# Gates of a token block: which PSUM buffers they use, and in which order gates, norm rows, output transposes and hidden splits are written

## The chip, the cores and the metric

The kernel runs on one core of one Trainium2 chip. The metric is the device time of one launch in microseconds (us), lower is better; the runs shown give its median.

## The reference, cut to what matters

One decoder layer for 1024 prompt rows and 32 sampled rows (8 sequences of 4), 1056 token rows in all, D_MODEL = 1024, D_FF = 2816. Attention, a state-space branch and their merge come first and are not touched here. What follows is:

```
up = rmsnorm(x, g_ffn) @ w_up
conv = conv_b + sum of three taps of up along the sequence
a, v = split(conv)
x = x + (gelu(a) * v) @ w_down
x = x + sigmoid(rmsnorm(x, g_ple) @ w_ple_gate) * (p @ w_ple_proj)
```

The last rows of `up` before the convolution are outputs as well (conv_prompt, conv_sample). All matrix products are done to fp32 accuracy.

## The kernel before, in words

**Products.** An fp32 operand is split in two fp32r parts, hi = round(x) and lo = x - hi. ACT casts the hi part (line 82), DVE or POOL subtracts (line 83). `mm3` (lines 85 to 88) then issues three matmuls per 128x128 weight tile: hi-hi, hi-lo, lo-hi. Activations lie transposed, features on partitions and tokens on columns.

**Up.** For each of 22 pairs of feature tiles, `up_pair` makes seven products (in the sequence `ORDER`), adds them to the quarters of `up`, runs the convolution and the gelu, and writes the hidden rows to the DRAM tensor `dhid` (`middle`). In the last pair `last_pair` begins to read the hidden rows of the first token block back: `hid_split(b, g, eng)` splits group g (three feature tiles, 128x1056; group 7 has one, 128x352) of block b into its fixed M tiles. Group 6 is called after the product m = 4, group 7 after the last pair's convolution and gelu.

**Blocks.** The tokens are cut in three blocks of 352 columns. `block(b)` does all of a block's remaining work:

- `down(o, kgs)`: for each of eight output tiles o, 22 feature tiles in six groups kg of four (the last of two), accumulated in a PSUM tile `pd` of the pool `psDn` (three buffers). `down_out` adds the residual (DVE, line 2157), scales by g_ple and splits into `GG[o]` (ACT 2160, DVE 2161), and adds the square to `sqb` (ACT 2166; POOL, or DVE for o = 7, 2167). In block 0 outputs 0 and 1 are interleaved.
- `gate(o)`: 8 k-tiles of `GG` in two groups kg, 24 matmuls, into a PSUM tile `pu` of the pool `psU` (three buffers).
- `sums` (line 2196): column sums of `sqb` by six small matmuls, then the reciprocal root on DVE (`rst`). `rows` (2208, 2209): transposes `rst` to a row on all partitions, which DVE copies to `rb`.
- `rest(o)`: DVE multiplies the gate by `rb` (2222), ACT takes the sigmoid (2223), DVE multiplies by the projected p in `pe[o]` and adds the residual (2224, 2225). The result is `y`.
- `out_turn(o)`: three transposes on TensorE into a tile `pt` of the pool `psP` (two buffers), two copies to SBUF on ACT (2234, 2236), and two DMA issues on ACT's queue (2235, 2238); a third (2240) in the last block.
- `hid_split(b + 1, o, V)` after gate o: the hidden rows of the next block.

In the order of the program: gate 0, sums, gate 1, rows, rest 0, rest 1, turn 0, gate 2, rest 2, turn 1, and so on. While outputs 2 and up of block 0 go through `down`, `last_rows` turns the conv rows of the outputs (lines 2125 to 2131), with one buffer for its SBUF tile `lo_`.

**Loads.** Weights and hidden rows share five SBUF buffers with the tag `raw`. `raw_load` lists the loads in order (`rseq`), `pull` issues the next one on SP's queue for each one that has been used up, so that five are loaded ahead; a hidden group is held back until its rows have been written. `raws` finds a loaded tile by its key: ("d", o, i) for a part of w_down, ("g", o) for w_ple_gate, ("h", b, g) for hidden rows. In the list, gate weights and hidden groups alternate: g0, h0, g1, h1, to g7, h7, then the next block's w_down.

**Weight units.** `units` lists the half loads in the order of their use, `dn_unit` splits one, and `ahead` keeps three split units in `wq` before TensorE's use of them. The split tiles have four buffers. The subtraction alternates between POOL and DVE.

**What sets the order.** The program's order is a priority. A planner issues on each engine the first instruction whose operands are ready and whose buffer is free in its own model of the times, and fixes the sequence of every engine's queue by that; each engine then works through its queue in that sequence and waits where an operand is late. So an instruction may stand on its engine ahead of others that the program names earlier.

Of the kernel before, what the change touches and what calls it, by code (L numbers as in the profile page):

```python
# [9 lines left out]
F32 = mybir.dt.float32  # L10
# [11 lines left out]
BLK = T // 3  # L22
# [33 lines left out]
def body(tc, I, O):  # L56
# [8 lines left out]
    with ctx:  # L65
# [1620 lines left out]
        units = []  # L1686
        for b in range(3):
            kgs = [(o, kg) for o in range(8) for kg in range(6)]
            if b == 0:
                kgs = [(o, kg) for q in (range(4), (4, 5)) for o in range(2) for kg in q] + kgs[12:]  # L1690
            units += [("d", o, kg) for o, kg in kgs] + [("g", o, kg) for o in range(8) for kg in range(2)]

        for b in range(3):
            if b == 0:
                for x in ("h0", (0, 0), "h1", "h2", (0, 1), "h3", "h4", "h5", "h6", (1, 0), (1, 1), (0, 2), "h7", (1, 2)):
                    if x[0] == "h":
                        hid_raw(0, int(x[1]))
                    else:
                        dn_load(*x)
            for o in range(2 if b == 0 else 0, 8):  # L1700
                for i in range(3):
                    dn_load(o, i)
            for o in range(8):
                raw_load(("g", o), k8(), w_pg[:, :, cols_(o)])
                if b < 2:
                    hid_raw(b + 1, o)

# [387 lines left out]
        def last_pair(m):  # L2095
            if m in ORDER[:6]:
                g = ORDER.index(m)
                hid_split(0, g, V if g % 2 else G)
            if m == 4:
                hid_split(0, 6, V)  # L2100
# [3 lines left out]
        while post:  # L2104
            step()
        hid_split(0, 7, V)
        pX.close()
# [16 lines left out]
        def last_rows(q):  # L2124
            pt = ps.tile([128, 512], F32, name="pt")
            for j in range(4):
                PE.transpose(pt[:18, j * 128:(j + 1) * 128], LU[:, q + j], ident)
            lo_ = p2.tile([18, 512], F32, name="lo_", bufs=1)
            A.copy(lo_, pt[:18])
# [5 lines left out]
        def block(b):  # L2135
# [10 lines left out]
            def p_in(o):  # L2146
                pe[o] = btile("pe", 3)
                SP.dma_start(pe[o], dpp[cols_(o), c])
# [34 lines left out]
            if b == 0:  # L2183
                for kgs in (range(4), (4, 5)):
                    for o in range(2):
                        down(o, kgs)
            for o in range(2 if b == 0 else 0, 8):
                down(o, range(6))
# [21 lines left out]

            def gate(o):
                pg_ = psu.tile([128, BLK], F32, name="pu")
                for kg in range(2):
                    wt = wq.pop(0)
                    ahead()
                    for k in range(4 * kg, 4 * kg + 4):
                        mm3(pg_, wt[:, 0, k % 4], wt[:, 1, k % 4], GG[k][:, 0], GG[k][:, 1], k == 0, k == 7)
                return pg_

            def rest(o, pg_):  # L2220
                y = Y[o] = btile("y", 3)
                V.tensor_tensor(y, pg_, rb, OP.mult)
# [18 lines left out]

            pgs = {}
            p_in(0)
            p_in(1)
            for o in range(8):
                pgs[o] = gate(o)
                if b < 2:
                    hid_split(b + 1, o, V)
                if o == 0:
                    rst = sums()  # L2250
                    continue
                if o == 1:
                    rows(rst)
                    rest(0, pgs.pop(0))
                rest(o, pgs.pop(o))
                if o < 7:
                    p_in(o + 1)
                out_turn(o - 1)
            out_turn(7)
# [44 lines left out]
```

## Time and profile before

| | us |
|---|---|
| median of 3 runs | 2057.62 |
| lowest, highest | 2054.71, 2059.20 |
| the profiled execution, its own time | 2064.64 |
| its span, from the first to the last instruction | 2062.8 |
| its mean granted TensorE clock, as a share of full speed | 0.968 |

All rows below come from the one profiled execution; times count from the start of its span. PE is TensorE's matmuls, DVE VectorE, ACT ScalarE, POOL GpSimd, SP the queue that issues most loads; a q behind an engine's name is its sequencer, which issues DMAs. `raw<-dhid` reads: into the tile raw, from dhid. In a timeline a row gives start, duration, engine, line of the kernel, operation, tiles and shapes, and in brackets how long the engine had been idle and what released it. A matmul row of 0.32 us overlaps the next one's by half. In these rows the up stage ends at about 1673 us, and the three blocks end at about 1814, 1938 and 2063 us.

### The profile page before, as it was taken

The numbers are of one execution on the slowest core, as the hardware profiler recorded it, in microseconds if no ns is written. First come the engines' busy times: TensorE is split into PE (matmuls) and PEld (weight loads), VectorE is DVE, ScalarE is ACT, GpSimd is POOL, SyncE is SP. The second block draws the span as 40 slices with busy tenths as digits, with TensorE's granted clock in tenths as the row PEclk, the third lists the DMA queues.
The fourth block names the chain that finished last, engine by engine and source line by source line (L and its number), as shares of the span: only waits on it lengthen the run. The fifth ranks groups of instructions, "written<-read, shape, count | busy, mean of one in ns | idle before, by whom it ended". The sixth has DMA issues, their size and how long they took to land.

```text
span 2062.8 us, 35870 instructions
## 1 busy us (share of the span) xinstructions
PE 1958.3 (95%) x13329; PEld 1839.7 (89%) x13329; DVE 1255.5 (61%) x2467; ACT 920.8 (45%) x1910; POOL 870.2 (42%) x926
## 2 busy tenths in 40 slices
PE   7998999999998989999999899999999989999998
PEld 6897888888777768888999899999999989999998
DVE  6517542335787856565553878787878773734524
ACT  5412332243665544455333454444444454544543
POOL 1106341101323222212442668787878754344342
PEclk9999999998999979999999999999999999999999
DMA  7402221243321100003356432322232274766743
GB/s 250 127 15 59 66 70 55 72 115 110 104 58 45 45 1 12 2 1 139 109 148 214 124 131 63 94 63 94 63 94 63 94 212 139 219 188 180 225 138 102
DMA packets 291927, 211.53 MB, mean 103 GB/s; under 512 B 38417, under 2 KB 273092, under 8 KB 291754
## 3 DMA queue, kind: packets, MB, share of 16 engines
q1 hardware_dynamic: 275102, 195.86, 32.0%
q10 hardware_dynamic: 16652, 13.39, 2.0%
q8 instruction: 105, 1.72, 0.3%
q14 instruction: 68, 0.56, 0.1%
HBM read 161.07 MB, written 46.78 MB: 101 GB/s over the span
## 4 chain that ended last, share of the span: by engine, by line
PE 74%; DVE 10%; ACT 2%; DMA 2%; POOL 2%; issue 2%; SPq 0%; ACTq 0%; DVEq 0%; POOLq 0%
PE q L2014 21%; PE pd L87 4%; PE pd L88 4%; PE pd L86 4%; PE q L1941 3%; PE pm L88 3%; PE pm L87 3%; PE pm L86 3%; PE pt L86 2%; PE pv L1377 2%; PE pt L88 2%; PE pt L87 2%; PE p L86 2%; PE p L88 2%; PE p L87 2%
## 5 line engine op out<-in xcount | busy, mean ns | idle before, releaser
L2014 PE MATMUL q<-M,wx 128*128 128x264 f32 x2112 | 279.2, 285 | 2.0 <-DVE up L2034 2.0
L2014 PEld LDWEIGHTS q<-M,wx 128*128 128x128 f32 x2112 | 266.8, 188 | 2.2 <-issue 2.2
L83 POOL TENSOR_TENSOR wx<-raw,wx 128x512 fp32r<-128x512 f32 x108 | 147.9, 1371 | 226.6 <-ACT wx L82 217.1
L82 ACT CAST wx<-raw 128x512 fp32r<-128x512 f32 x226 | 133.5, 597 | 195.4 <-PE pd L88 117.1
L2014 PE MATMUL q<-P,wx 128*128 128x264 f32 x1584 | 216.0, 285 | 0.1
L2014 PEld LDWEIGHTS q<-P,wx 128*128 128x128 f32 x1584 | 200.3, 188 | 3.8 <-DVE up L2026 3.8
L83 DVE TENSOR_TENSOR wx<-raw,wx 128x512 fp32r<-128x512 f32 (+1 forms) x118 | 92.2, 783 | 141.1 <-ACT wx L82 137.6
L86 PE MATMUL pd<-M,wx 128*128 128x352 f32 x528 | 171.8, 325 | 0.0
L87 PE MATMUL pd<-M,wx 128*128 128x352 f32 x528 | 171.4, 325 | 0.0
L88 PE MATMUL pd<-M,wx 128*128 128x352 f32 x528 | 171.2, 324 | 0.0
L2057 DVE SCALAR_TENSOR_TENSOR cv<-up,cw,cv 128x1024 f32<-128x1024 f32 x88 | 142.1, 1615 | 28.3 <-ACT cv L2049 28.3
L88 PE MATMUL pm<-xh,wl 128*128 128x352 f32 x384 | 126.9, 331 | 0.0
L87 PE MATMUL pm<-xl,wh 128*128 128x352 f32 x384 | 126.5, 329 | 0.0
L86 PE MATMUL pm<-xh,wh 128*128 128x352 f32 x384 | 126.1, 328 | 0.0
L1359 POOL TENSOR_TENSOR Pt<-Pt,mstT 128x128 f32<-128x128 f32 x64 | 30.6, 480 | 176.4 <-ACT Pt L1358 176.4
L86 PEld LDWEIGHTS pd<-M,wx 128*128 128x128 f32 x528 | 100.0, 189 | 0.1
L87 PEld LDWEIGHTS pd<-M,wx 128*128 128x128 f32 x528 | 99.9, 189 | 0.0
L88 PEld LDWEIGHTS pd<-M,wx 128*128 128x128 f32 x528 | 99.9, 189 | 0.0
L1747 ACT CAST wx<-raw 128x512 fp32r<-128x512 f32 x110 | 67.9, 618 | 71.4 <-PE q L2014 46.5
L1941 PE MATMUL q<-M,wx 128*128 128x264 f32 x720 | 90.8, 286 | 5.4 <-POOL wx L83 2.6
L1941 PEld LDWEIGHTS q<-M,wx 128*128 128x128 f32 x720 | 88.3, 188 | 6.8 <-POOL wx L83 3.1
L1748 DVE TENSOR_TENSOR wx<-raw,wx 128x512 fp32r<-128x512 f32 x66 | 76.5, 1159 | 11.8 <-ACT wx L1747 11.8
(705 smaller groups left out, 5473.3 us busy)
## 6 DMA issues: line engine op xcount, KB each, us to landing
raw<-w_down SPq DMA_DIRECT2D x48, 512.0 KB
raw<-w_up SPq DMA_DIRECT2D x44, 512.0 KB
raw<-w_ple_gate SPq DMA_DIRECT2D x24, 512.0 KB
dhid<-cv SPq DMA_DIRECT2D x22, 528.0 KB
raw<-dhid SPq DMA_DIRECT2D x21, 528.0 KB
raw<-w_down SPq DMA_DIRECT2D x24, 384.0 KB
wst<-w_in SPq DMA_DIRECT2D x16, 512.0 KB
cb<-cache_ckv SPq DMA_DIRECT2D x64, 128.0 KB
```

The lines of the kernel that those rows point to most:

```text
L82: A.copy(hi, src)
L83: (eng or G).tensor_tensor(lo, src, hi.bitcast(F32), OP.subtract)
L86: PE.matmul(out, lh, rh, start=start, stop=False)
L87: PE.matmul(out, lh, rl, start=False, stop=False)
L88: PE.matmul(out, ll, rh, start=False, stop=stop_)
L1359: G.tensor_tensor(Pt[:, :128], Pt[:, :128], mstT, OP.add)
L1377: PE.matmul(W["pv"][:, j, :DV + 1], Pts[k][:, q0:q0 + 128], Vb[hp][:, k, e], start=k == 0, stop=k == i)
L1747: A.copy(w[:, 0], s)
L1748: (G if m in (2, 5, 4) else V).tensor_tensor(w[:, 1], s, w[:, 0].bitcast(F32), OP.subtract)
L1941: PE.matmul(p_[:, n, :QW], a_, b_[:, k % 4], start=k + x == 0 and kg == 0, stop=k == 7 and x == 2)
L2014: PE.matmul(o_, l_, r_, start=start and k + x == 0, stop=k + x == 5, skip_group_check=not start)
L2057: V.scalar_tensor_tensor(C[:, :S], U[:, tp:tp + S], w[tp], C[:, :S], op0=OP.mult, op1=OP.add)
```

## The change

Gates 0 and 1 are computed together, first their k-tiles 0 to 3, then 4 to 7, and the list of weight units follows. Gate 3 and gate 7 take a PSUM tile of psDn, the others of psU. The sums stand behind gates 0 and 1, the rows behind gate 3, followed by rest 0, 1 and 2. From gate 4 on, gate o is followed by rest o - 1, a hidden split of the next block and the turn of output o - 3 (for o = 4 also of output 0); the turns of outputs 5, 6 and 7 stand behind gate 7 and its rest. Hidden splits of the next block begin after rest 2, and their loads are listed accordingly: g0 to g3, h0, h1, g4, h2, g5, h3, g6, h4, g7, h5, h6, h7. In the last up pair group 6 is split after the product m = 3, and group 7 of block 0 after the first four kg of down outputs 0 and 1. `pe` and `y` get four buffers in place of three, `lo_` three in place of one, and pe[2] is loaded at the start.

```diff
@@ -1688,7 +1688,7 @@
             kgs = [(o, kg) for o in range(8) for kg in range(6)]
             if b == 0:
                 kgs = [(o, kg) for q in (range(4), (4, 5)) for o in range(2) for kg in q] + kgs[12:]
-            units += [("d", o, kg) for o, kg in kgs] + [("g", o, kg) for o in range(8) for kg in range(2)]
+            units += [("d", o, kg) for o, kg in kgs] + [("g", o, kg) for op in ((0, 1), (2,), (3,), (4,), (5,), (6,), (7,)) for kg in range(2) for o in op]
 
         for b in range(3):
             if b == 0:
@@ -1702,8 +1702,9 @@
                     dn_load(o, i)
             for o in range(8):
                 raw_load(("g", o), k8(), w_pg[:, :, cols_(o)])
-                if b < 2:
-                    hid_raw(b + 1, o)
+                for g in {3: (0, 1), 7: (5, 6, 7)}.get(o, (o - 2,) if o > 3 else ()):
+                    if b < 2:
+                        hid_raw(b + 1, g)
 
         wsum = {}
 
@@ -2096,14 +2097,13 @@
             if m in ORDER[:6]:
                 g = ORDER.index(m)
                 hid_split(0, g, V if g % 2 else G)
-            if m == 4:
+            if m == 3:
                 hid_split(0, 6, V)
 
         for j in range(NH):
             up_pair(j, first_pair if j == 0 else last_pair if j == NH - 1 else lambda m: None)
         while post:
             step()
-        hid_split(0, 7, V)
         pX.close()
         f1.close()
 
@@ -2125,7 +2125,7 @@
             pt = ps.tile([128, 512], F32, name="pt")
             for j in range(4):
                 PE.transpose(pt[:18, j * 128:(j + 1) * 128], LU[:, q + j], ident)
-            lo_ = p2.tile([18, 512], F32, name="lo_", bufs=1)
+            lo_ = p2.tile([18, 512], F32, name="lo_", bufs=3)
             A.copy(lo_, pt[:18])
             A.dma_start(cvp[:, q * 128:(q + 4) * 128], lo_[0:2])
             A.dma_start(cvs[:, q * 128:(q + 4) * 128], lo_[2:18])
@@ -2144,7 +2144,7 @@
                 SP.dma_start(xb[o], dx2[cols_(o), c])
 
             def p_in(o):
-                pe[o] = btile("pe", 3)
+                pe[o] = btile("pe", 4)
                 SP.dma_start(pe[o], dpp[cols_(o), c])
 
             def down_group(pd, kg):
@@ -2184,6 +2184,8 @@
                 for kgs in (range(4), (4, 5)):
                     for o in range(2):
                         down(o, kgs)
+                    if 0 in kgs:
+                        hid_split(0, 7, V)
             for o in range(2 if b == 0 else 0, 8):
                 down(o, range(6))
                 for _ in range(3):
@@ -2208,17 +2210,20 @@
                     PE.transpose(pt[:, t0:t0 + n], rst[:n, i:i + 1].to_broadcast([n, 128]), ident[:n, :n])
                 V.tensor_copy(rb, pt[:, :BLK])
 
-            def gate(o):
-                pg_ = psu.tile([128, BLK], F32, name="pu")
+            pgs = {}
+
+            def gate(os_):
+                for o in os_:
+                    pgs[o] = psd.tile([128, BLK], F32, name="pd") if o % 4 == 3 else psu.tile([128, BLK], F32, name="pu")
                 for kg in range(2):
-                    wt = wq.pop(0)
-                    ahead()
-                    for k in range(4 * kg, 4 * kg + 4):
-                        mm3(pg_, wt[:, 0, k % 4], wt[:, 1, k % 4], GG[k][:, 0], GG[k][:, 1], k == 0, k == 7)
-                return pg_
+                    for o in os_:
+                        wt = wq.pop(0)
+                        ahead()
+                        for k in range(4 * kg, 4 * kg + 4):
+                            mm3(pgs[o], wt[:, 0, k % 4], wt[:, 1, k % 4], GG[k][:, 0], GG[k][:, 1], k == 0, k == 7)
 
             def rest(o, pg_):
-                y = Y[o] = btile("y", 3)
+                y = Y[o] = btile("y", 4)
                 V.tensor_tensor(y, pg_, rb, OP.mult)
                 A.activation(y, y, AF.Sigmoid)
                 V.tensor_tensor(y, pe[o], y, OP.mult)
@@ -2239,23 +2244,36 @@
                 if m < 96:
                     A.dma_start(ysv[:, oc], yo[m:96, 2])
 
-            pgs = {}
+            def rows_in(g):
+                if b < 2:
+                    hid_split(b + 1, g, V)
+
             p_in(0)
             p_in(1)
-            for o in range(8):
-                pgs[o] = gate(o)
-                if b < 2:
-                    hid_split(b + 1, o, V)
-                if o == 0:
-                    rst = sums()
-                    continue
-                if o == 1:
-                    rows(rst)
-                    rest(0, pgs.pop(0))
+            p_in(2)
+            gate((0, 1))
+            rst = sums()
+            gate((2,))
+            p_in(3)
+            gate((3,))
+            rows(rst)
+            for o in range(3):
                 rest(o, pgs.pop(o))
-                if o < 7:
-                    p_in(o + 1)
-                out_turn(o - 1)
+            rows_in(0)
+            for o in range(4, 8):
+                p_in(o)
+                gate((o,))
+                rest(o - 1, pgs.pop(o - 1))
+                rows_in(o - 3)
+                if o == 4:
+                    out_turn(0)
+                out_turn(o - 3)
+            rest(7, pgs.pop(7))
+            rows_in(5)
+            out_turn(5)
+            rows_in(6)
+            out_turn(6)
+            rows_in(7)
             out_turn(7)
 
         for b in range(3):
```

## Rows read from the trace of the kernel before

**Rows 1.** The page, its first line.
```profile
span 2062.8 us, 35870 instructions
```

**Rows 2.** Windows: us; busy (x) of five engines; PEclk, DMA share, GB/s.
```profile
1700.00:1762.00 62.00, 62.00 (x399) 60.95 (x398) 22.09 (x31) 30.71 (x57) 28.58 (x24) 1.00 0.52 146
...
1772.00:1782.00 10.00, 7.64 (x30) 6.85 (x29) 8.72 (x21) 4.76 (x7) 2.78 (x3) 0.67 0.74 221
...
1925.00:1938.00 13.00, 12.35 (x81) 12.03 (x79) 8.00 (x14) 7.03 (x16) 4.09 (x4) 1.00 1.05 307
```

**Rows 3.** Waits of PE, 1671 to 2063 us: total us, times, longest.
```profile
PE pt L2232 <- DVE y L2225: 5.6, 6, 2.1
PE pt L2127 <- ACT lo__19576 L2129: 4.3, 1, 4.3
PE pt L2196 <- DVE sqb L2167: 2.0, 2, 1.0
PE pu L87 <- DVE gg L2161: 1.4, 2, 0.7
PE pu L86 <- ACT gg L2160: 1.0, 2, 0.6
PE pt L2208 <- DVE rst L113: 0.9, 1, 0.9
```

**Rows 4.** Timeline, PE and ACT, end: start, us, engine, line, [idle before].
```profile
2055.67 0.49 PE L2232 MATMUL pt<-ident,y 128*128 128x128 f32 x3
...
2056.20 0.37 ACT L2234 COPY yo<-pt 128x256 f32<-128x256 f32 x1 [3.08 <-PE pt L2232]
...
2058.23 0.52 PE L2232 MATMUL pt<-ident,y 128*128 128x128 f32 x3 [2.07 <-DVE y L2225]
...
2058.78 0.37 ACT L2234 COPY yo<-pt 128x256 f32<-128x256 f32 x1 [1.49 <-PE pt L2232]
...
2060.15 0.59 ACTq L2240 DMA_DIRECT2D y_sample<-yo  x1
```

**Rows 5.** Timeline, DVE, before the first block's gates.
```profile
1770.96 1.26 DVE L83 TENSOR_TENSOR M<-raw,M 128x1056 fp32r<-128x1056 f32 x1 [2.59 <-ACT M L82]
1772.14 0.51 DVE L2157 TENSOR_TENSOR xb<-pd,xb 128x352 f32<-128x352 f32 x1
```

**Rows 6.** Timeline, ACT and SP, hidden rows around the first block's gates.
```profile
1760.23 1.07 ACT L82 CAST M<-raw 128x1056 fp32r<-128x1056 f32 x1
...
1773.98 0.37 SPq L1655 DMA_DIRECT2D raw<-dhid  x1
...
1779.03 1.07 ACT L82 CAST M<-raw 128x1056 fp32r<-128x1056 f32 x1 [3.27 <-DMA raw<-dhid]
```

**Rows 7.** Timeline, PE, first block's gates.
```profile
1777.97 0.49 PE L88 MATMUL pu<-gg,wx 128*128 128x352 f32 x1
...
1778.26 0.49 PE L86 MATMUL pu<-gg,wx 128*128 128x352 f32 x1
...
1782.30 0.32 PE L88 MATMUL pu<-gg,wx 128*128 128x352 f32 x1
```

**Rows 8.** Timeline, PE and DVE, the last block's rows of the norm.
```profile
2028.92 0.46 PE L2208 MATMUL pt<-ident,rst 128*128 128x128 f32 x3
...
2029.42 0.53 DVE L2209 COPY rb<-pt 128x352 f32<-128x352 f32 x1 [1.41 <-PE pt L2208]
...
2030.46 0.95 DVE L2222 TENSOR_TENSOR y<-pu,rb 128x352 f32<-128x352 f32 x2
```

**Rows 9.** Timeline, all engines, from up to down.
```profile
1677.77 1.25 DVE L83 TENSOR_TENSOR M<-raw,M 128x1056 fp32r<-128x1056 f32 x1
...
1678.93 0.64 PE L86 MATMUL pd<-M,wx 128*128 128x352 f32 x1
...
1695.78 1.17 ACT L82 CAST wx<-raw 128x512 fp32r<-128x512 f32 x2 [1.66 <-DMA raw<-w_down]
...
1696.47 1.29 POOL L83 TENSOR_TENSOR wx<-raw,wx 128x512 fp32r<-128x512 f32 x1 [3.67 <-ACT wx L82]
```

## The prediction

> **What bounds the kernel now.** I read the span first [rows 1], then busy time by stage [rows 2], who made TensorE wait in the last 392 us [rows 3], and then single stretches. The reader is to see that TensorE sets the pace: while a down product runs it is busy without a break at full clock, 399 matmuls in 62 us, one each 0.16 us, and the other engines have slack. Time is to be had only where TensorE stands still or runs at half clock, and in what follows its last matmul. In the gates that is twelve waits besides the final one [rows 3]: 5.6 us for y less the final 2.1 [rows 4], 2.0 us for the sum of squares, 1.4 and 1.0 us for the two halves of the last gg, 0.9 us for rst; 8.8 us. One more, 4.3 us for a copy of conv rows on ACT, lies at the switch from up to down.
>
> Two things lie behind these rows. The split of a hidden group stands on DVE ahead of the residual add of the last down output: DVE waits 2.59 us for it, works 1.26 us, and only then comes L2157 [rows 5]; so the last gg and the sum of squares are late. And such splits run as soon as their rows land, not where the program names them: one is cast at 1760.23 us, 12 us before L2157 [rows 5, 6].
>
> **The change, part by part.** The profiled execution took 2064.64 us around a span of 2062.8 us, 7.0 us over the median of the runs, 2057.62 us. I work out the difference on it and carry it over to the median.
>
> *Waits taken away.* The k=7 products of the first gates come after 33 matmuls, not 21; at 0.16 us that is 5.3 us in place of 3.4 us after the last down matmul. With the first hidden load now behind four gate weights, L2157 no longer queues behind a split; from it to the last half of gg there are three operations on the same 352 columns, and its row is 0.51 us [rows 5], so some 2 us with the gaps, an estimate. The sum stands behind 48 matmuls, rst has two more gates (7.7 us) instead of one, and most outputs are turned three gates after their own. I let all twelve waits go. Each costs 0.16 us more than its idle time, because a matmul's row of 0.32 us overlaps the next by half: 8.8 + 12 x 0.16 = 10.7 us; bounds 6 and 10.7. In the first block the stop also cost the clock: between 1777.97 and 1782.30 us matmuls follow each other every 0.29 us, 15 of them, at 0.16 us 2.4 us [rows 7]; 1.9 us. The granted clock was 0.67 in that stretch [rows 2]. Together 12.6 us.
>
> *A wait put in.* Output 4 takes the PSUM buffer of output 0: of psU's three, 0, 1 and 2 hold all, and only 3 and 7 go to psDn. That buffer is free after rest(0)'s product with rb, and rb now comes after the fourth gate. So TensorE, done with the rows' transposes, waits for DVE's copy and product. In the last block of before, the transposes began at 2028.92, the copy ended at 2029.95, and two products took 0.95 us from 2030.46, behind another operation of DVE [rows 8]. To the end of the first product, about 0.5 us in, are 2.0 us, without the other operation 1.5 us; less 0.3 us of TensorE's own transposes, 1.7 or 1.2 us. With a hidden split in between, 1.26 us [rows 5], it would be 2.5 us. I take 1.3 us in the last block, which has no hidden splits, and 1.8 us in the other two: 4.9 us; bounds 3.6 and 7.5. All later gates and transposes are queued behind the waiting gate, so nothing covers it. The Trainium skill, "Perfetto Trace Analysis", section Matmuls, says that independent groups should rotate through different PSUM banks, so that one is evacuated under the matmuls of the next. By that rule a fifth gate in one of psDn's idle buffers would not wait and the gain would be 4.9 us larger; no run here shows it.
>
> *What stays.* DVE still splits hidden groups between the products for y, and at a block's end four outputs are turned with two transpose buffers. Of waits of up to 0.7 us I leave 0.8 us in each of the first two blocks: 1.6 us; bounds 0 and 4.
>
> *The end.* Before, two output turns follow the last gate; after, four: 4, 5, 6 and 7. One turn occupies ACT from 2058.78 to 2060.74 us with two copies and three DMA issues, 1.96 us [rows 4]. Before, ACT's first copy begins 0.53 us after the last gate's matmuls and its last issue ends 5.07 us after them. With four turns and the last sigmoid (some 0.5 us, one more pass over 352 columns) that is 0.53 + 4 x 1.96 + 0.5 = 8.87 us, 3.8 us more. Two turns' transposes, 0.65 us, leave TensorE's stream before. Loss 3.1 us; bounds 0, were turns 4 and 5 issued within the last gate, and 3.8.
>
> *The switch.* The third group of conv rows waits on TensorE for ACT's copy [rows 3], so down begins only at 1678.93 [rows 9]. Moving group 6's split behind the last up product takes 1.25 us of DVE [rows 9] out of the chain that ends in the last hidden rows; more buffers for the conv rows let ACT copy sooner. But little of that wait can be won: the first load of weights behind the last hidden rows on SP's queue feeds the 115th down matmul, and its split ends at 1697.76 us [rows 9], while that matmul stands at 1678.93 + 14 x 0.29 + 100 x 0.16 = 1699.0. The slack is 1.2 us; with 1.25 us from DVE the limit is 2.5 us. I take 1.5 us of gain; bounds a loss of 1 and 2.5. Group 7's split moves behind eight down units, but its rows are written by the last up pair and land after that anyway: 0.
>
> *Edits at nothing.* Four buffers for pe and y and one load of pe more at the start: a load of 176 KB hides behind two gates; without that cover it would be late by what a landing takes, 5.05 us at most [rows 6]. Eight weight loads and eight hidden loads change places on SP's queue, none is added.
>
> Sum: 12.6 - 4.9 - 1.6 - 3.1 + 1.5 = 4.5 us. The profiled execution would be 2060.1 us, the median 2053.1 us.
>
> **The rivals.**
> (a) *One raw buffer less: slower.* Loads run five entries ahead of use. When the first down unit of the next block is built, at the second unit of gate 6, eight gate weights and now only three hidden groups have been used: 11 + 5 = 16 entries are loaded, and w_down (0, 0) is the 17th. Its key carries no block, so the unit finds the tile of the block before, the same numbers, which therefore stays alive through a whole block. Five raw buffers become four in the first two blocks. In the down stage four buffers of 3.9 us each outlast a load. In the gates a weight load could then wait for the one before it: 5.05 us from the issue of a 528 KB load to its cast [rows 6], and some 1.9 us for a cast, half of 1.17, and POOL's split of 1.29 [rows 9], 7.0 us, against 4.2 us for an output. That is 2.8 us per output; for two outputs in each of two blocks 11.2 us, so 6.7 us slower than before: 2064.3 us. For it: DMA is already full in the late gates, share 1.05 [rows 2]. Against it: hidden splits run when they land [rows 6], so their buffers come back early. It decides once a weight waits for another weight rather than for a hidden group.
> (b) *Nothing to measure.* The planner puts a hidden split ahead of the rows' copy on DVE, as it stood ahead of L2157 [rows 5]. The wait at the fifth gate is then 2.5 us in two blocks and 1.3 in one, half the old waits for y come back (3 us), and the switch gives nothing: 12.6 - 6.3 - 3.0 - 3.1 = 0.2 us: 2057.4 us. For it: that order in the first block of before. Against it: the first hidden loads come later now.
> (c) *The whole gain.* The edit does not do what it says in two places, to its good: the planner issues the rows within gate 3 and turns 4 and 5 within gate 7. Then 12.6 - 1.6 + 1.5 = 12.5 us: 2045.1 us. Against it: TensorE follows the program while its operands are ready.
>
> **How the numbers follow.** Forecast 0.50 with its own range 2049 to 2057, (a) 0.18, (b) 0.15, (c) 0.17. The range 2045 to 2062 leaves out half of (c) and most of (a). About 0.2%, 4.1 us, is what a measurement of this kernel can tell from no change; below 2053.5 counts as faster. The forecast lies at that edge, six parts in ten beyond it: faster 0.30 + 0.17 = 0.47; same 0.18 + 0.13 = 0.31; slower 0.18 and what is left of the others, 0.22.
>
> **What would show it.** Right: no wait of TensorE for gg, sqb or rst; one wait of 1 to 2 us before the fifth gate of each block, put down to DVE's product with rb; no half clock near the first gates; four turns on ACT behind the last gate and 10 to 11 us from its last matmul to the end. Wrong: waits of gates for weight splits, the mark of (a); a fifth gate that starts behind the rows without a wait, the mark of (c); a switch that gives more than 2.5 us, which would mean that the load behind the last hidden rows does not set it.

## The result, and the profile after

The changed kernel took 2072.59 us (median of 5 runs, 2067.16 to 2075.57) against 2058.24 us for the kernel before in the same set (5 runs, 2054.71 to 2059.29): ratio 1.0065, 95% interval 1.0045 to 1.0086. It is slower by some 14 us. The forecast was a gain of 4.5 us, and the range, up to 2062, did not hold the time.

The two profiled executions differ by only 3.2 us, 2067.81 against 2064.64. Their up parts, in which the change edits nothing but one call in the last pair, differ by 10.5 us the other way (the last up matmul starts at 1662.27 us, before at 1672.78). From that matmul to the end of the span it is 403.8 us after and 390.0 us before: 13.8 us more, which agrees with the medians. Every kernel below is compared by this length, beside its ratio.

The stages, from the first to the last matmul of each by its start (the switch: from the last up matmul to the first of down; the end: from the last gate matmul's start to the end of the span; the sum: from the last up matmul to the end of the span). The sum also holds the steps between two stages, 0.2 to 1.9 us.

| us | switch | down 0 | gates 0 | down 1 | gates 1 | down 2 | gates 2 | end | sum |
|---|---|---|---|---|---|---|---|---|---|
| before | 6.2 | 90.1 | 41.2 | 85.0 | 38.6 | 85.6 | 34.9 | 7.3 | 390.0 |
| after | 5.3 | 91.0 | 40.2 | 91.2 | 39.1 | 89.0 | 34.9 | 11.3 | 403.8 |

The gates as a whole stay (114.7 and 114.2 us), the switch gains 0.8, and the loss is in the down stages, 10.5 us (9.6 of them in down 1 and 2), and at the end, 4.0 us.

The span of after, the first line of its page, answers to [rows 1]:

```profile
span 2066.0 us, 35832 instructions
```

What TensorE waited for after the up stage (total us, times, longest), beside [rows 3]:

```profile
PE pu L86 <- DVE y L2227: 10.5, 3, 4.5
PE pt L2127 <- ACT lo__19576 L2129: 4.1, 1, 4.1
PE pt L2237 <- DVE y L2230: 3.7, 2, 2.6
PE pt L2237 <- ACT yo L2241: 3.5, 2, 3.2
PE pd L86 <- ACT wx L82: 1.3, 1, 1.3
PE pd L88 <- POOL wx L83: 0.8, 1, 0.8
```

The waits for gg, sqb and rst of [rows 3] are gone. In their place stand three waits before the fifth gate, 10.5 us, and at the block ends waits for the turns' copies (yo) and for weight splits of w_down, which the kernel before did not have.

Windows of after (us; busy and count of PE, PEld, DVE, ACT, POOL; granted clock, DMA share, GB/s): the first two gates of block 0 with the sums, its fifth gate, its end, beside [rows 2].

```profile
1758.00:1769.00 11.00, 11.00 (x73) 11.00 (x72) 6.57 (x10) 6.39 (x10) 4.70 (x3) 1.00 0.45 142
...
1774.00:1786.00 12.00, 7.69 (x33) 7.48 (x32) 9.07 (x16) 6.85 (x11) 2.87 (x2) 0.72 0.82 261
1799.00:1810.00 11.00, 7.78 (x37) 7.39 (x36) 4.40 (x8) 3.94 (x12) 1.27 (x1) 0.69 1.03 302
```

The clock no longer falls at the first gates, as it did in [rows 2, 7] (1.00 in the first window); it falls behind the new waits (0.72 and 0.69 in the other two). The timeline of TensorE at the fifth gates of blocks 0 and 2 and at the end of block 0:

```profile
1774.74 0.47 PE L2210 MATMUL pt<-ident,rst 128*128 128x128 f32 x3
1779.52 0.63 PE L86 MATMUL pu<-gg,wx 128*128 128x352 f32 x1 [4.31 <-DVE y L2227]
1779.95 0.49 PE L87 MATMUL pu<-gg,wx 128*128 128x352 f32 x1
1780.24 0.49 PE L88 MATMUL pu<-gg,wx 128*128 128x352 f32 x1
...
1785.23 0.42 PE L87 MATMUL pu<-gg,wx 128*128 128x352 f32 x1
...
1798.87 0.32 PE L88 MATMUL pd<-gg,wx 128*128 128x352 f32 x1
...
1803.54 0.90 PE L2237 MATMUL pt<-ident,y 128*128 128x128 f32 x3 [3.22 <-ACT yo L2241]
...
2035.92 0.47 PE L2210 MATMUL pt<-ident,rst 128*128 128x128 f32 x3
2038.12 0.40 PE L86 MATMUL pu<-gg,wx 128*128 128x352 f32 x1 [1.74 <-DVE y L2227]
```

Behind the 4.31 us stop matmuls follow each other every 0.29 us until 1785.23 us, which costs 2.6 us more; in block 1, behind 4.46 us, 1.4 us more. The three fifth gates so cost 10.5 + 4.0 = 14.5 us.

DVE in the same stretch of block 0, and in the last block, beside [rows 5, 8]:

```profile
1773.53 1.26 DVE L83 TENSOR_TENSOR M<-raw,M 128x1056 fp32r<-128x1056 f32 x1 [1.00 <-ACT M L82]
1774.70 0.69 DVE L83 TENSOR_TENSOR wx<-raw,wx 128x512 fp32r<-128x512 f32 x1
1776.65 1.26 DVE L83 TENSOR_TENSOR M<-raw,M 128x1056 fp32r<-128x1056 f32 x1 [1.26 <-ACT M L82]
1777.82 0.52 DVE L2211 COPY rb<-pt 128x352 f32<-128x352 f32 x1
1778.26 0.68 DVE L83 TENSOR_TENSOR wx<-raw,wx 128x512 fp32r<-128x512 f32 x1
1778.86 1.38 DVE L2227 TENSOR_TENSOR y<-pu,rb 128x352 f32<-128x352 f32 x3
...
2036.42 0.53 DVE L2211 COPY rb<-pt 128x352 f32<-128x352 f32 x1 [2.81 <-PE pt L2210]
2036.86 0.68 DVE L83 TENSOR_TENSOR wx<-raw,wx 128x512 fp32r<-128x512 f32 x1
2037.46 1.38 DVE L2227 TENSOR_TENSOR y<-pu,rb 128x352 f32<-128x352 f32 x3
```

The reader is to see the order: the rows' transposes are done at 1775.2 us, but a hidden group's split stands on DVE ahead of the copy to rb and waits 1.26 us for its cast, so that the copy begins at 1777.82. That wait and the split, 2.5 us, on top of the last block's 1.74 us make the 4.3 us. In the last block, which has no hidden groups, the copy begins 0.03 us after the transposes. ACT's timeline shows what the cast waited for, and further on why block 0 ends late, beside [rows 6]; the last three rows are the end of the kernel, beside [rows 4]:

```profile
1775.54 1.07 ACT L82 CAST M<-raw 128x1056 fp32r<-128x1056 f32 x1 [0.69 <-DMA raw<-dhid]
...
1801.53 0.62 ACT L82 CAST wx<-raw 128x512 fp32r<-128x512 f32 x1 [2.91 <-DMA raw<-w_down]
...
1802.96 0.36 ACT L2239 COPY yo<-pt 128x256 f32<-128x256 f32 x1
...
2059.94 0.37 ACT L2239 COPY yo<-pt 128x256 f32<-128x256 f32 x1 [1.55 <-issue]
...
2062.02 0.37 ACT L2239 COPY yo<-pt 128x256 f32<-128x256 f32 x1 [1.55 <-issue]
...
2063.39 0.59 ACTq L2245 DMA_DIRECT2D y_sample<-yo  x1
```

A cast of w_down waits 2.91 us for its landing, and the copy of an output turn (1802.96) stands behind it on ACT, with TensorE waiting for that copy. SP's queue after the change issues its first w_down of the next block at 1793.18 us, 5.7 us ahead of the block's last gate matmul (1798.87):

```profile
1793.18 0.38 SPq L1655 DMA_DIRECT2D raw<-w_down  x1
```

Before, the same two points lie 12.0 us apart (the timelines of SP and of TensorE in the kernel before):

```profile
1798.36 0.38 SPq L1655 DMA_DIRECT2D raw<-w_down  x1
...
1810.32 0.32 PE L88 MATMUL pu<-gg,wx 128*128 128x352 f32 x1
```

### The profile page after: what moved, and what is told of

It is laid out like the page before. It is cut to its first block, busy times and chain, and to the rows that moved or that the text cites. A ratio compares the mean times of both kernels' runs of the same rounds, so it can differ in the third digit from the quotient of the medians.

```text
span 2066.0 us, 35832 instructions
## 1 busy us (share of the span) xinstructions
PE 1954.2 (95%) x13329; PEld 1839.0 (89%) x13329; DVE 1253.2 (61%) x2467; ACT 920.5 (45%) x1910; POOL 867.8 (42%) x926
## 4 chain that ended last, share of the span: by engine, by line
PE 75%; DVE 11%; DMA 4%; ACT 4%; issue 3%; POOL 2%; SPq 1%; ACTq 0%; DVEq 0%; POOLq 0%
PE q L2015 21%; PE pd L88 4%; PE pm L87 4%; PE pd L87 4%; PE pd L86 4%; PE pm L88 4%; PE pm L86 4%; PE q L1942 3%; PE pv L1377 2%; PE pt L86 2%; PE pt L88 2%; PE pt L87 2%; PE p L86 2%; PE p L88 2%; PE p L87 1%
## 5 line engine op out<-in xcount | busy, mean ns | idle before, releaser
L83 DVE TENSOR_TENSOR wx<-raw,wx 128x512 fp32r<-128x512 f32 (+1 forms) x118 | 87.7, 744 | 162.0 <-ACT wx L82 159.0
L1942 PEld LDWEIGHTS q<-M,wx 128*128 128x128 f32 x720 | 89.8, 191 | 6.5 <-POOL wx L83 2.8
```

Of the source, the lines that this page charges most:

```text
L83: (eng or G).tensor_tensor(lo, src, hi.bitcast(F32), OP.subtract)
L1942: PE.matmul(p_[:, n, :QW], a_, b_[:, k % 4], start=k + x == 0 and kg == 0, stop=k == 7 and x == 2)
```

## The experiments

Fifteen kernels. Sums and stages as in the table above, from one trace of each kernel; ratios to the kernel before, with 95% intervals. In the table, "3, own hidden buffers" means kernel 3 with that edit more.

| kernel | down 0 | gates 0 | down 1 | gates 1 | down 2 | gates 2 | end | sum | ratio |
|---|---|---|---|---|---|---|---|---|---|
| 1 after, no hidden groups | 90.0 | 34.9 | 86.6 | 34.9 | 85.4 | 34.9 | 11.3 | 383.7 | 0.9975 (0.9958, 0.9991) |
| 2 before, no hidden groups | 89.6 | 33.8 | 85.0 | 34.9 | 85.0 | 34.9 | 7.3 | 376.5 | 0.9945 (0.9926, 0.9964) |
| 3 after, gate 4 in psDn | 90.2 | 34.7 | 92.2 | 37.2 | 89.8 | 33.5 | 11.3 | 395.0 | 1.0032 (1.0016, 1.0048) |
| 4 after, hidden later still | 90.8 | 40.0 | 91.5 | 39.0 | 92.9 | 34.9 | 11.3 | 407.7 | 1.0078 (1.0055, 1.0100) |
| 5 3, hidden split on POOL | 90.1 | 40.4 | 94.2 | 44.7 | 90.3 | 33.5 | 11.3 | 410.6 | 1.0099 (1.0064, 1.0135) |
| 6 after, w_down (0, 0) earlier | 90.6 | 42.0 | 90.8 | 42.0 | 86.8 | 34.9 | 11.3 | 404.5 | 1.0070 (1.0037, 1.0104) |
| 7 3, own hidden buffers | 89.5 | 39.7 | 86.1 | 39.3 | 85.4 | 33.5 | 11.3 | 390.5 | 1.0007 (0.9990, 1.0024) |
| 8 3, hidden as before | 91.3 | 40.0 | 88.1 | 43.1 | 85.4 | 33.5 | 11.3 | 398.7 | 1.0055 (1.0037, 1.0073) |
| 9 3, two turns at the end | 90.9 | 37.3 | 89.3 | 36.4 | 88.4 | 34.3 | 9.4 | 395.8 | 1.0038 (1.0022, 1.0054) |
| 10 8 and 9 | 90.8 | 41.1 | 86.8 | 42.4 | 89.1 | 34.5 | 9.4 | 399.1 | 1.0048 (1.0026, 1.0071) |
| 11 before, switch | 90.1 | 39.5 | 85.0 | 40.7 | 85.0 | 34.9 | 7.3 | 387.9 | 1.0000 (0.9981, 1.0019) |
| 12 before, pairing | 89.5 | 44.2 | 85.1 | 45.2 | 85.0 | 36.2 | 7.3 | 398.4 | 1.0053 (1.0034, 1.0072) |
| 13 11, hidden three gates later | 91.0 | 39.0 | 87.9 | 41.3 | 87.1 | 34.9 | 7.3 | 395.5 | 1.0041 (1.0024, 1.0057) |
| 14 11, hidden one gate later | 91.0 | 37.5 | 84.9 | 41.6 | 84.9 | 34.9 | 7.3 | 388.7 | 0.9985 (0.9973, 0.9996) |
| 15 11, own hidden buffers | 90.2 | 39.5 | 85.0 | 41.7 | 85.0 | 34.9 | 7.3 | 388.5 | 1.0014 (0.9996, 1.0031) |

How far single traces agree: the kernel before and 11 have the same code from the first gate on, and their gates 0 and 1 differ by 1.7 and 2.1 us. The switch, new in fourteen of the traces, took 3.7 to 5.5 us in them, and 4.7 to 6.2 us in the three with the old code. Sums and ratios agree within 3 us, in 15 within 4.4. Down 1 and 2 are steadier: 84.9 to 85.1 us in 2, 11, 12, 14 and 15. So a difference of up to 2 us in the gates or at the switch, from two traces, shows no effect by itself.

**1 and 2. Without hidden groups.** The hidden rows of blocks 1 and 2 are neither loaded nor split. Two lines go, the one in the load list and the split:

```diff
-                        hid_raw(b + 1, g)
+                        pass
-                    hid_split(b + 1, g, V)
+                    pass
```

In the changed kernel:

> The changed kernel without the loads and splits of the hidden groups of blocks 1 and 2: those blocks multiply block 0's hidden rows again. Theory (the hidden groups make both losses, the wait at the fifth gate and the late w_down): gates of blocks 0 and 1 take 35 us as in the last block, from 40.2 and 39.1, with a fifth gate's wait of 2.0 us; down stages 85 to 87 us; together 19 us less, about 385 us from the last up matmul to the end. Rival (the sequence of gates, rows and turns is the cause): more than 392 us.

In the kernel before:

> The kernel before without the same loads and splits. Theory: gates of blocks 0 and 1 take 35 us, from 41.2 and 38.6, as in its last block; 10 us less, about 380 us from the last up matmul to the end. Set against the run before this one it gives what the edits are worth where no hidden group is in the way: by the last block's rows, 0 us for a block's gates and a loss of 4 us at the end. Rival (its waits are those of the last gg and of the sums and remain without hidden groups): 386 us or more.

Waits of TensorE, the changed kernel without hidden groups, then the kernel before without them:

```profile
PE pu L86 <- DVE y L2226: 5.2, 3, 1.7
PE pt L2236 <- DVE y L2229: 3.3, 2, 2.6
```

```profile
PE pt L2230 <- DVE y L2223: 3.9, 3, 2.1
```

Both theories held, the second with 13.5 us in place of 10. The fifth gate now costs 1.7 us in every block with no half clock behind it, so 14.5 - 5.2 = 9.3 us of its price is the hidden groups' doing, and down 1 and 2 are back at 85 to 87 us. These kernels drop loads, casts and splits at once; which of the three it is they do not say. Hidden groups cost the changed kernel 403.8 - 383.7 = 20.1 us and the kernel before 390.0 - 376.5 = 13.5 us. And 383.7 - 376.5 = 7.2 us of the loss do not need them: 4.0 at the end, 2.4 in the down stages, 1.2 in gates 0, 0.6 between the stages, less 1.0 at the switch.

**3. Gate 4 in an idle PSUM buffer.**

```diff
-if o % 4 == 3 else
+if o in (3, 4, 7) else
```

> The changed kernel, with gate 4 in an idle buffer of psDn, too. Theory (the fifth gate waits only for the PSUM buffer of output 0): the waits before it, 4.5, 4.7 and 2.0 us, go with the half clock behind two of them, 4.0 us; 12 to 15 us in all, 2057 to 2060 us, and the sixth gate does not wait, since the product of output 1 comes one pass of 0.5 us after that of output 0. Rival (the rows' copy and the products are late on DVE, and the turns of outputs 0 and 1 behind gate 4 wait for y in place of the gate): half of it comes back, 2064 to 2067 us.

The rival had it closer, 2066.1 us. Its waits:

```profile
PE pt L2237 <- DVE y L2230: 6.0, 4, 2.6
PE pt L2237 <- ACT yo L2241: 5.6, 3, 3.5
...
PE pu L86 <- DVE y L2227: 0.3, 1, 0.3
```

The gate waits 0.3 us in place of 10.5; the gates fall by 8.7 us in all, of the 14.5. What is left comes as turns that wait for y (two stops of 1.1 and 1.9 us in blocks 0 and 1). The down stages stay late.

**4 and 5. Where the splits stand on DVE.** In 4 every hidden group is loaded one gate later; the splits keep their places in the program:

```diff
-for g in {3: (0, 1), 7: (5, 6, 7)}.get(o, (o - 2,) if o > 3 else ()):
+for g in {4: (0, 1), 7: (4, 5, 6, 7)}.get(o, (o - 3,) if o > 4 else ()):
```

> The changed kernel (gate 4 in psU) with every hidden group listed one gate later: h0 and h1 behind g4, h4 to h7 behind g7. Theory (hidden splits that wait for their late loads stand on DVE ahead of the rows' copy): the waits at the fifth gates of blocks 0 and 1 fall from 4.5 and 4.7 us to about 2.0 us, what the last block has without hidden groups, and their half clock with them, 7 to 9 us less in the gates; the down stages of blocks 1 and 2 grow by 2 to 6 us, since w_down comes later yet. Rival (the gate waits for DVE's copy and product alone, whatever is beside them): the waits stay within 0.5 us of 4.5.

The first part of the theory fell: the gates stay at 40.0 and 39.0, and TensorE waits 4.1 and 4.5 us before their fifth gates. That is the number of the rival, but not its reason: without hidden groups the same copy and product cost 1.7 us (1). ACT's timeline, then DVE's, show that loading a group later does not take it out of the way:

```profile
1781.52 1.07 ACT L82 CAST M<-raw 128x1056 fp32r<-128x1056 f32 x1 [2.99 <-DMA raw<-dhid]
...
1782.63 1.26 DVE L83 TENSOR_TENSOR M<-raw,M 128x1056 fp32r<-128x1056 f32 x1 [1.56 <-ACT M L82]
1783.80 0.52 DVE L2211 COPY rb<-pt 128x352 f32<-128x352 f32 x1
```

Its cast waited 2.99 us for the rows, and the copy to rb still stands behind. The second part, 2 to 6 us more in the down stages, held for block 2 (3.9 us), not for block 1 (0.4 us). In 5 the subtraction goes to POOL, on top of 3:

```diff
-                    hid_split(b + 1, g, V)
+                    hid_split(b + 1, g, G)
```

> The changed kernel with gate 4 in psDn, and with the subtraction of the hidden groups of blocks 1 and 2 on POOL in place of DVE. Theory (splits that wait for late rows stand on DVE ahead of the rows' copy): the turns behind the fifth and sixth gates, 1.4 and 2.2 us late, wait less than 0.7 us each, as in the last block; gates of block 1 fall from 37.2 to 34 to 35 us; 2 to 4 us less, 2062 to 2064 us. Rival (POOL takes 1.29 us for a split of 512 columns, so about 2.6 us for one of 1056, and splits half of the weights): gates wait for POOL's wx, 2 to 6 us more.

Neither: it is the slowest of all, and not for want of POOL's weights (0.8 us of waits in all). DVE's small operations on 128x3 elements, mostly 0.16 us each, become long while POOL subtracts; DVE, then POOL:

```profile
1768.66 2.18 DVE L99 TENSOR_SCALAR rf_i<-msx 128x3 int32<-128x3 int32 x1
...
1774.07 0.16 DVE L113 SCALAR_TENSOR_TENSOR rf_i<-rf_a,rf_i 128x3 f32<-128x3 f32 x1
...
1774.46 2.31 DVE L111 TENSOR_TENSOR rf_a<-rf_a,msx 128x3 f32<-128x3 f32 x1
...
1778.42 2.39 DVE L113 SCALAR_TENSOR_TENSOR rst<-rf_a,rf_i 128x3 f32<-128x3 f32 x1
```

```profile
1765.47 5.34 POOL L83 TENSOR_TENSOR M<-raw,M 128x1056 fp32r<-128x1056 f32 x2 [2.34 <-ACT M L82]
...
1774.27 2.48 POOL L83 TENSOR_TENSOR M<-raw,M 128x1056 fp32r<-128x1056 f32 x1 [0.45 <-ACT M L82]
...
1778.39 2.41 POOL L83 TENSOR_TENSOR M<-raw,M 128x1056 fp32r<-128x1056 f32 x1 [0.41 <-ACT M L82]
```

rst comes late, and the rows' transposes wait 5 us for it in blocks 0 and 1.

**6 and 7. Why w_down is late.** In 6 the next block's w_down (0, 0) is listed ahead of h7 and left out of its old place:

```diff
+                        if g == 7:
+                            dn_load(0, 0)
                         hid_raw(b + 1, g)
...
-                for i in range(3):
+                for i in range(0 if o or b == 0 else 1, 3):
```

The expectation says ahead of the last three groups; the edit puts it ahead of the last one alone. That makes it the sixteenth entry in place of the seventeenth, and so within the sixteen that are loaded when its unit is built.

> The changed kernel, with the next block's first w_down load listed ahead of the last three hidden groups, so that the unit that uses it finds the new tile and no raw buffer is held through a block. Theory (one raw buffer less, rival a): the late w_down loads at the ends of blocks 0 and 1 go; the down stages of blocks 1 and 2, 91.2 and 89.0 us after the change, fall to 85 to 87 us as before it; some 7 us in all, about 2065 us. Rival (the sequence of the loads and of ACT's casts sets it, not the number of buffers): both down stages stay within 2 us of 91.2 and 89.0; 2070 to 2073 us.

The rival's numbers, 2073.97 us: down 1 stays, down 2 gains 2.2 us, and the gates lose 4.7. One buffer held through a block is, by itself, not the cause of the loss; how a still earlier place would do was not tried. In 7, on top of 3, the hidden groups of blocks 1 and 2 get two SBUF buffers of their own. The line that allocates them, out of a longer edit:

```diff
+                t = raws["h", b, g] = p2.tile([128, 3 * BLK], F32, name="hraw", bufs=2)
```

> The changed kernel with gate 4 in psDn (2066.1 us, 395.0 us from the last up matmul to the end), and with two SBUF buffers of their own for the hidden groups of blocks 1 and 2, so that the five raw buffers hold weights alone. Theory (hidden groups hold raw buffers behind the last gate, so that w_down is late): the down stages of blocks 1 and 2, 92.2 and 89.8 us, fall to 85 to 87 us; 8 to 10 us less, 2056 to 2058 us. Rival (the sequence on ACT's and DVE's queues sets it): they stay within 2 us, 2064 to 2068 us.

The down stages fall as the theory has it, by 6.1 and 4.4 us: the raw buffers that hidden groups hold at a block's end are what makes w_down late (its first load is now issued 23.7 us ahead of block 0's last gate matmul, in 3 it was 1.6 us). The gates lose 7.0 us of it. Groups now start earlier and still land late, ahead of the sums on DVE; ACT's timeline in block 0, then DVE's:

```profile
1774.05 1.08 ACT L82 CAST M<-hraw 128x1056 fp32r<-128x1056 f32 x1 [4.55 <-DMA hraw<-dhid]
```

```profile
1772.45 0.17 DVE L100 TENSOR_SCALAR rf_i<-rf_i 128x3 int32<-128x3 int32 x1
1775.16 1.26 DVE L83 TENSOR_TENSOR M<-hraw,M 128x1056 fp32r<-128x1056 f32 x1 [2.53 <-ACT M L82]
1776.33 0.16 DVE L110 SCALAR_TENSOR_TENSOR rf_a<-rf_i 128x3 f32<-128x3 f32 x1
```

The reciprocal root stands still for 3.7 us in the middle of its steps, 2.5 of them with DVE idle.

**8, 9 and 10. Hidden groups as before, and fewer turns at the end.** On top of 3. In 8 the list and the calls alternate again, one group behind each gate from the first on:

```diff
-                for g in {3: (0, 1), 7: (5, 6, 7)}.get(o, (o - 2,) if o > 3 else ()):
-                    if b < 2:
-                        hid_raw(b + 1, g)
+                if b < 2:
+                    hid_raw(b + 1, o)
```

> The changed kernel with gate 4 in psDn (the run before this one, 2066.1 us, 395.0 us from the last up matmul to the end), and with the hidden groups loaded and split one per gate from the first gate on, as in the kernel before. Theory (three hidden groups behind the last gate hold three of five raw buffers, so that w_down is late at a block's end): the down stages of blocks 1 and 2, 92.2 and 89.8 us, return to 85 to 87 us, 9 to 12 us less; the gates lose 1 to 4 us of it, because splits stand ahead of the rows' copy on DVE again; 2057 to 2061 us. Rival (four turns on ACT hold the casts up): the down stages stay within 2 us of 92.2 and 89.8, 2066 to 2070 us.

The down stages gave 8.5 us back, near the theory's 9 to 12, but the gates took 11.2 where 1 to 4 were expected; 2067.07 us. In 9:

```diff
-                if o == 4:
-                    out_turn(0)
-                out_turn(o - 3)
+                for t in {4: (0, 1), 5: (2, 3), 6: (4,), 7: (5,)}[o]:
+                    out_turn(t)
```

> The changed kernel with gate 4 in psDn, and with outputs 2 and 3 turned behind gate 5, 4 behind gate 6, 5 behind gate 7, so that two turns follow the last gate, as before, not three or four. Theory (late loads of w_down): only the end returns, 11.3 to 7.5 us, and the down stages of blocks 1 and 2 stay above 88 us; 3 to 5 us less, 2061 to 2063 us. Rival (the turns on ACT): those stages fall to 85 to 87 us as well; 2052 to 2056 us.

The end gained 1.9 us, not 3.8. The down stages of blocks 1 and 2 fell by 2.9 and 1.4 us and stayed above 88: the late loads set most of it, the turns on ACT a part. The gates and the steps behind them lost 4.9 us, since turns now wait for y ten times, 9.7 us, in place of four times, 6.0 us, and the whole is no shorter. Both together, 10:

> Both edits: gate 4 in psDn, hidden groups one per gate as in the kernel before, two turns behind the last gate. If the losses add, the two before this taken together: 395.0 less 8 less 4, 383 us from the last up matmul to the end, against 390.0 for the kernel before; 2050 to 2055 us, faster than both kernels. If turns and splits only change places on DVE and ACT, 2056 to 2060 us.

They do not add: 399.1 us, 16 more than the first case, and 2066.5 us is above the second as well. Down 2 stays at 89.1 us although its first w_down is issued 18.8 us ahead of the last gate matmul; a turn at its start waits 2.2 us for y.

**11 and 12. Two parts of the change alone, on the kernel before.** In 11 the edits at the switch, as in the diff of the change:

> The kernel before with only the edits at the switch: group 6 after m = 3, group 7 behind the first eight down units, three buffers for the conv rows. My forecast: 1.5 us less from the last up matmul to the end of the span, 390.0 to 388.5 us. The changed kernel's trace: 0.8 us less there. Rival: nothing, or a loss of 1 us, because the split of group 7 comes late for the ninth down unit. The median between 2055.5 and 2059.

2.1 us less in the trace (the switch itself 4.2 us, from 6.2), nothing that the runs can tell. In 12 gates 0 and 1 are paired, the sums stand behind them and the rows behind gate 2:

```diff
+                if o != 1:
+                    gate((0, 1) if o == 0 else (o,))
...
+                if o == 2:
+                    rows(rst)
```

> The kernel before with only gates 0 and 1 together, the sums behind them and the rows behind gate 2; loads, hidden splits, PSUM buffers and most turns as before. Theory (pairing takes the waits for gg, the sum of squares and rst, and the half clock): 6 to 7 us less, about 2051.5 us, with no wait of TensorE for gg or sqb. Rival (a hidden split still stands on DVE ahead of the last residual add, 2.6 us late, and the pairing's 1.9 us more cover does not reach): waits for gg of 1 us remain in each block, and gate 3 waits for the buffer of output 0, 1.5 us each; no gain, 2055 to 2060 us.

The theory fell, and of the rival only one half came, larger than it said: the waits for gg and sqb are gone, but with the hidden groups where they were rst is late by 3.1 and 3.2 us, and the fourth gate waits for output 0's buffer 7.7 us in three blocks, 1.7 of them in the last. Pairing alone loses 8.4 us.

**13, 14 and 15. Hidden groups in the sequence of before.** On top of 11. In 13 they have the places of the changed kernel:

> The kernel before with the edits at the switch and the hidden groups listed and split as in the changed kernel, three gates later; gates, rows, PSUM buffers and turns as before. Theory (their place alone moves the loss): gates of blocks 0 and 1 fall from 39.5 and 40.7 to 34 to 36 us, the down stages of blocks 1 and 2 grow from 85.0 to 88 to 92 us; in all 384 to 392 us. Rival (the four turns behind the last gate make the down stages late): those stay at 85 to 86 us, and the whole falls to 378 to 381 us, faster than both kernels by some 9 us.

The down stages grow by 2.9 and 2.2 us, and the gates do not fall; turns that follow their output by one gate wait for y nine times, 13.3 us. Their place alone loses 395.5 - 387.9 = 7.6 us, 2.0 of it at the switch and in down 0, which the edit does not touch. The first w_down of block 1 leads by 5.2 us, no more than the 5.7 us of the changed kernel:

```profile
1793.51 0.38 SPq L1655 DMA_DIRECT2D raw<-w_down  x1
...
1798.68 0.32 PE L88 MATMUL pu<-gg,wx 128*128 128x352 f32 x1
```

In the changed kernel, with its four turns behind the last gate, the down stages are another 3.3 and 1.8 us longer (91.2 and 89.0 us): late loads alone do not explain them. In 14:

```diff
-                    hid_raw(b + 1, o)
+                    for g in ((6, 7) if o == 7 else (o - 1,) if o else ()):
+                        hid_raw(b + 1, g)
```

and the same for the splits.

> The kernel before with the edits at the switch (387.9 us from the last up matmul to the end, gates 39.5 and 40.7 us in blocks 0 and 1) and every hidden group one gate later in the list and in the program. Theory (later hidden groups leave the gates and come into the down stages): gates of blocks 0 and 1 fall by 1 to 3 us each, to 37 to 39 us, and the down stages of blocks 1 and 2, 85.0 us both, grow by less than 1 us; 384 to 386 us. Rival (a group blocks DVE wherever it stands): gates unchanged within 1 us, 387 to 390 us.

2053.36 us, ratio 0.9985 (0.9973 to 0.9996): the only complete kernel of the fifteen whose interval lies below the kernel before, by about 3 us. The interval just misses 1, and one such among thirteen can come by chance. Its profile doesn't show where a gain would lie: against 11, gates 0 gained 2.0 us, gates 1 lost 0.9, and from the last up matmul it is 1.3 us below before and 0.8 above 11 (1.2 below 11, if counted from the first gate). In 15 two buffers of their own, as in 7:

> The kernel before with the edits at the switch and two SBUF buffers of their own for the hidden groups of blocks 1 and 2. Theory (a group's landing, not its buffer, holds up DVE in the gates; the down stages had no loss): nothing, 386 to 390 us. Rival (groups wait for raw buffers in the gates): gates of blocks 0 and 1 fall to 35 to 37 us; 380 to 383 us, faster than both kernels.

As the theory has it, no gain: in the sequence of before, buffers were not what the groups waited for.

## Why the prediction was wrong

**Waits taken away: right, together with the other edits.** The waits for gg, sqb and rst and the half clock at the first gates are gone. The gates changed by -0.5 us with 14.5 us of new cost in them, so 15.0 us left them; two turns a block, 0.65 us each time, went to the next stage or the end, which leaves 13.0 us against the forecast 12.6 (0.8 of that for a wait outside the gates). But the pairing gives this only where no hidden group stands near the sums: alone it lost 8.4 us (12).

**A wait put in: the first step that failed.** The prediction put 4.9 us on the fifth gates, with 7.5 as the upper bound; they cost 14.5. Place and releaser were right. In the last block, 1.3 us was taken and 1.7 measured, since a weight split stands between copy and product there. In the other two its worst case was one hidden split in between, 1.26 us of work. What the rows show is a split that itself waits for its cast, and the cast for its landing, ahead of the copy, so that DVE stands idle in front of work that is ready. Rival (b) named that order and priced it at 2.5 us; 4.3 and 4.5 came. Without hidden groups it is 1.7 in each block (1). The half clock behind two of the waits, 4.0 us, was in no term. The rule of the Trainium skill cited there, that independent groups rotate through PSUM banks ("Perfetto Trace Analysis", section Matmuls), agrees with experiment 3: the gate's wait fell from 10.5 to 0.3 us, and the sum by 8.8.

**What stays: the second step that failed,** 1.6 us forecast with bounds of 0 and 4; the down stages lost 10.5. "Eight weight loads and eight hidden loads change places on SP's queue" was put at nothing. They also change who holds the five raw buffers when the last gate runs: w_down is then issued 5.7 us ahead of the last gate matmul in place of 12.0, its casts block ACT, and the turns' copies stand behind them. It takes both the late loads and the four turns on ACT: against the 85.0 us of 11, down 1 and 2 are 2.9 and 2.2 us longer with late loads alone (13), 1.1 and 0.4 with four turns alone (7, own buffers), and 7.2 and 4.8 with both (3). Seen from 3, own buffers take 10.5 us away (7), fewer turns 4.3 (9).

**Rival (a)** has the time nearest to the result and the wrong mechanism: its mark, gates that wait for weight splits, is absent, and with the first w_down load earlier (6) the whole is no faster. **Rival (c)** did not occur: no fifth gate without a wait.

**The end: right.** The span ends 11.3 us after the last gate matmul starts, 4.0 us later than before; less the 0.65 us of turns that left the last gates, that is 3.4 us against 3.1 forecast, with four turns on ACT, the last two 2.08 us apart. **The switch: not decided.** 1.5 us was forecast; 0.8 in the changed kernel and 2.0 alone (11) lie within the scatter of single traces, and the ratio of 11, 1.0000 (0.9981 to 1.0019), can tell neither from nothing. That the load behind the last hidden rows limits it was not tried.

What stays open: that DVE's sequence follows from rows that the planner's model takes to land earlier than they do is argued from the waits on DMA, not shown; whether and where experiment 14 gains; and whether any place of the hidden groups reaches the 376.5 us of experiment 2.

## What to carry to other kernels

Before moving a load in a list, count who holds each shared buffer at the moment that the next stage's first load should start: a move that is free in bytes can halve the lead of the loads behind it. A wait that the change adds costs what stands on the releasing engine's queue ahead of the release, including that work's own wait for a DMA; price it with the worst queue seen in the trace, and add the half clock that followed the stops of 3.2 us and more here. Moving work off the path paid nothing here as long as the same late rows stood in front of it on an in-order engine; try the kernel without those loads first, which shows in one run how much there is to win.

## What the runs showed of the hardware

DVE's operations on 128x3 elements mostly took 0.16 us, and three took 2.18 to 2.39 us when they met one of POOL's subtractions of 128x1056 (2.48 and 2.41 us, and two in 5.34); a weight split of DVE, 0.69 us, took 2.54 us beside them (5). Each of the three ended within 0.03 us of POOL's own end. In the changed kernel the same happened on a smaller scale: two of the eleven such operations of block 0 took 1.02 and 1.19 us beside POOL's weight splits. The Trainium skill, "SBUF — State Buffer", section "Who interferes with whom", says that the two engines share a pair of SBUF ports, for DVE's instructions with two inputs in SBUF or in a two-port mode, and that the one that comes second is blocked for the whole of the other's instruction; these rows agree, down to operations of three elements a partition. Work moved to POOL was therefore not off DVE's path.

TensorE's clock fell to its lower level, 1.2 of 2.4 GHz, behind some of its stops and not behind others: in the changed kernel matmuls followed every 0.29 us behind those of 4.31, 4.46 and 3.22 us, with a mean granted clock of 0.72 and 0.69 in the windows around the first and the last of these, and every 0.16 us behind the one of 1.74 us. Nor did the longest single stop decide it in the kernel before: three stops of 0.64, 0.71 and 1.02 us at the first gates of block 0 ended at half clock [rows 7], while 0.34, 0.71 and 1.02 us in block 1 left the granted clock at 1.00 (1900 to 1905 us).
